# Staging the turned convolution blocks in the filter tiles, and moving their reads and the second heads' values into the next head

## The chip, the cores and the metric

One core of a Trainium2 chip runs the whole layer. It has five engines with a queue each: TensorE (PE in the profile; its weight loads are listed as PEld), VectorE (DVE), ScalarE (ACT), GpSimd (POOL) and SyncE (SP). They run side by side and wait for one another by semaphores; transfers are issued from the queues of SP, ACT and POOL. The metric is the device time of one execution in microseconds, the median of three runs.

## The reference

A decoder layer for 256 tokens of 2048 channels in float32. Two mixers work side by side on the normalised input, 16 heads of attention and a short gated convolution; their projections are gated, added, and projected once more. Cut to what matters:

```python
q_nope, q_rope, k_nope, k_rope, v = ...      # from two 512-wide latents, 16 heads
attn = causal_softmax(q k^T * scale) @ v     # per head: 256 x 256 scores
attn = attn * silu(z_mla)
y_mla = attn @ w_o_mla

u = c_gate * c_in
u_pad = jnp.pad(u, ((0, 0), (CONV_K - 1, 0), (0, 0)))
conv = sum(conv_w[k] * u_pad[:, k:k + s] for k in range(CONV_K))
y_conv = (b_gate * conv * silu(z_conv)) @ w_o_conv

merged = sigmoid(g_mla) * y_mla + sigmoid(g_conv) * y_conv
x = x + rmsnorm(merged @ w_out)
```

## The kernel before

Every product is made to float32 accuracy from two rounded parts: a tile is split into a high part (a copy on ScalarE) and a low part (a subtraction on VectorE) by `split_act` (L232), and three matmuls go for one. The weights come in units of 128 x 2048 (1 MB) through three `raw` buffers on SP's queue, and each unit is split in two halves into `whi` and `wlo`, five buffers each (L186). TensorE's order is written out by hand (`matmul` at L88 keeps program order). For VectorE and ScalarE a scheduler at build time sets the order, save where an instruction is kept in program order; the transfers of POOL discussed here are all kept.

The change lies in the loop over 16 heads (L743 to L804). Each head also carries a sixteenth of the convolution's projections: head h = 4j + n makes the n-th of four products (c_gate, c_in, z_conv, b_gate, in that order) of the j-th block of 512 channels, in four quarters `channels(h, 0..3)` of 24 matmuls. `channels_done` (L689) folds each product into the block in `cv_f` or into `cv_w`. A block has two token halves t of 128 tokens, `cv_t[:, j, t, :]`.

A head from h = 2 on runs so: the gate `z` (`project`, `silu`), `scores(h)`, the quarters of the convolution, with `values` and some steps between, then in odd heads up to 13 the queries and keys of the next pair (`group_a`: matmuls `qn` and `kn`), in heads 3, 7 and 11 the values of the next four heads (`vv`), in even heads `qr`, and the last quarter.

- `scores(h)` (L590) multiplies queries and keys, masks, and makes the softmax in the tile `p` (one buffer).
- `turned(src, via, n)` (L304) turns a tile by a round trip through DRAM: VectorE transposes 32 x 32 blocks into the staging tile `via` (L308); `go` (L311) issues four DMAs from POOL's queue that write it to the tile `far` in DRAM (L315); `come` (L317) issues one DMA from POOL's queue that reads it back (L319) and must wait for the four writes. For `p` the `go` stands in `scores`, the `come` in the loop behind the second quarter.
- `turn(h, p)` (L635) splits the turned scores into `pt` (one buffer), ScalarE's copy and VectorE's subtraction kept in program order.
- `values(h, pt, sz)` (L648) multiplies `pt` by the head's values: four matmuls into the bank `o`, then a copy on ScalarE and an addition and a multiplication on VectorE into `at_f`. In even heads `turn` stands at the end, behind `channels(h, 3)`, and `values` in the next head behind its first quarter. In odd heads both stand in the head itself: `turn` behind the third quarter, `values` behind `group_a`.
- `taps(j, t)` (L706) is the convolution itself for a block's token half, in three parts run at different places: shifted copies of the block into the tiles `mv1` and `mv2` (one buffer each) and two filter rows into tiles `cw` (two buffers), then the products with these and their sum, and the third filter row into `cw`; then the last product and sum. The second half t = 1 starts at the end of head 4j + 1 and is summed in head 4j + 2; the first half t = 0 starts at the end of head 4j + 3 and is summed in head 4j + 4 (the last block's in heads 14 and 15).
- `channels_join(j, t)` (L701) multiplies the convolved block by its gate and turns it in place with `turned_back` (L323): transpose, four writes and the read, one behind the other in POOL's queue. It runs for t = 1 at the end of heads 3, 7, 11 and 15, for t = 0 at the end of heads 4, 8 and 12 and behind the loop. The turned blocks are used after the last head only, in `split_channels` (L825).

All turned tiles of the loop share one staging buffer `via` of 512 columns (L334), but for the very last block, which uses `mv2`.

Of the kernel before, what the change touches and what calls it, by code (L numbers as in the profile page):

```python
# [18 lines left out]
P = 128  # L19
# [63 lines left out]
def tile_layer(ctx: ExitStack, tc: tile.TileContext, xw, x, pos, pvec, post_g, wc, wz, wcv, wkr, wqk, wqr, wv, cwr, wsq, out):  # L83
# [119 lines left out]
    def take(i):  # L203
        ahead(i)
        parts = splits.pop(i)

        def piece(j, n):
            o = j * n
            h, o = o // HALF, o % HALF
            return parts[h][0][:, o : o + n], parts[h][1][:, o : o + n]  # L210

        return piece

    def bank(name, tag="mm", bufs=4):
        return psum.tile([P, 512], F32, name=name, tag=tag, bufs=bufs)

    def product(ps, a, b, first, last):

        (ah, al), (bh, bl) = a, b
        matmul(ps, ah, bh, start=first, stop=False)  # L220
        matmul(ps, ah, bl, start=False, stop=False)
        matmul(ps, al, bh, start=False, stop=last)
# [69 lines left out]
    n = 2 * XW // S  # L292
# [3 lines left out]
    def temp(name, shape=(P, S), dt=F32, bufs=2, tag=None):  # L296

        tag, n = tag or name.rstrip("0123456789_"), shape[-1]
        if n % LINE == 0:
            return bp.tile(list(shape), dt, name=name, tag=tag, bufs=bufs)  # L300
        return bp.tile([P, -(-n // LINE) * LINE], dt, name=name, tag=tag, bufs=bufs)[:, :n]


    def turned(src, via, n):  # L304

        via = via[:, : P * n]
        v = via.rearrange("p (q k x) -> p q k x", q=4, k=n)
        nc.vector.transpose(v.rearrange("p q k x -> p k q x"), src)  # L308
        far = dram.tile([P, P * n], F32, name="far", tag=f"far{n}", bufs=2)

        def go():  # L311
            f = far[:, :].rearrange("(q y) (i m) -> i y q m", q=4, i=4)
            for i in range(4):
                m = via[32 * i : 32 * i + 32, :].rearrange("y (q m) -> y q m", q=4)
                tc.keep_in_program_order(nc.gpsimd.dma_start(out=f[i], in_=m))  # L315

        def come(dst):  # L317

            tc.keep_in_program_order(nc.gpsimd.dma_start(out=dst, in_=far[:, :]))  # L319

        return go, come

    def turned_back(src, via, n):  # L323
        go, come = turned(src, via, n)
        go()
        come(src)

    def by_rows(t, n):
        return t.rearrange("p (i k x) -> p k i x", i=4, k=n)

    def quarters(t):
        return t.rearrange("p k (i x) -> p k i x", i=4)

    def via():  # L334
        return temp("via", (P, 512), bufs=1)


    def split_scaled(dst, src, k):
# [248 lines left out]
    def make(i, j):  # L587
        {"a": group_a, "r": group_r, "v": group_v}[i](j)

    def scores(h):  # L590

        (qn, kn), qr = groups["a", h // HG], groups["r", h // HG]
        j = h % HG
        sc = bank(f"sc{h}", tag="st", bufs=1)
        t0, t1 = slice(0, P), slice(P, S)
        mm = matmul
        o = sc[:, :S].rearrange("p (i k) -> p i k", i=2)
        mm(o, qn[0][:, j, t0], kn[:, :, j, :P], start=True, stop=False)
        mm(sc[:, :P], qn[1][:, j, t0], kn[:, 0, j, :P], start=False, stop=False)
        mm(o, qr[:, j, t0], kr[:, :, :P], start=False, stop=True)  # L600
        o = sc[:, S:]
        product(o, [a[:, j, t1] for a in qn], [kn[:, i, j, :] for i in range(2)], True, False)
        for i in range(2):
            mm(o, qr[:, j, t1], kr[:, i, :], start=False, stop=i == 1)
        if h == 0:
            temp("pad", (P, 4 * LINE), bufs=1)
        p = temp("p", (P, 3 * P), bufs=1)
        half = temp("sc_half", (P, P), bufs=1)
        nc.scalar.activation(half[:, :], sc[:, P:S], AF.Copy)
        nc.vector.tensor_tensor(p[:, :P], sc[:, :P], half[:, :], op=ALU.add)  # L610
        nc.vector.tensor_tensor(p[:, :P], p[:, :P], mask[:, :P], op=ALU.add)
        nc.vector.tensor_tensor(p[:, P:], sc[:, S:], mask[:, P:], op=ALU.add)
        mx, sm, rs = temp("mx", (P, NT)), temp("sm", (P, NT)), temp("rs", (P, NT))
        nb = temp("nb", (P, NT))
        for t in range(NT):
            o = slice(t * P, (2 * t + 1) * P)
            nc.vector.reduce_max(mx[:, t : t + 1], p[:, o], axis=mybir.AxisListType.X)
        nc.vector.tensor_scalar(nb[:, :], mx[:, :], -SCALE, None, op0=ALU.mult)
        for t in range(NT):
            o = slice(t * P, (2 * t + 1) * P)  # L620
            nc.scalar.activation(
                p[:, o], p[:, o], AF.Exp, bias=nb[:, t : t + 1], scale=SCALE,
                accum_out=sm[:, t : t + 1],
            )
        nc.vector.reciprocal(rs[:, :], sm[:, :])
        for t in range(NT):
            o = slice(t * P, (2 * t + 1) * P)
            nc.vector.tensor_scalar(p[:, o], p[:, o], rs[:, t : t + 1], None, op0=ALU.mult)
        if h < 2:
            return p, None  # L630
        go, come = turned(p[:, :], via(), 3)
        go()
        return p, come

# [27 lines left out]
    def silu(name, ps):  # L662
        f, s = temp("sl_f", bufs=1), temp(name)
        whole(f[:, :], ps)
        rows(f[:, :])
        nc.scalar.activation(s[:, :], f[:, :], AF.Sigmoid)
        nc.vector.tensor_tensor(s[:, :], f[:, :], s[:, :], op=ALU.mult)
        return s
# [5 lines left out]
    def channels(h, i, between=None):  # L674

        if i == 0:
            cv_ps["now"] = [bank(f"cv{h}_{t}", tag="cv", bufs=2) for t in range(NT)]
        w = take(u_head[h][1 + i])
        for t in range(NT):
            if t and between:  # L680
                between()
            for k4 in range(4):
                k = 4 * i + k4
                a = [x_both[:, k, o + t * P : o + (t + 1) * P] for o in (0, S)]
                product(cv_ps["now"][t][:, :], a, w(k4, 512), k == 0, k == KD - 1)
        if i == 3:
            channels_done(*divmod(h, 4))
# [13 lines left out]
    def channels_join(j, t):  # L701
        u, w = cv_t[:, j, t, :], cv_w[:, t, :]
        nc.vector.tensor_tensor(u, u, w, op=ALU.mult)
        turned_back(u, via() if t or j < 3 else temp("mv2", (P, 512), bufs=1, tag="mv2x"), 4)

    def taps(j, t):  # L706

# [31 lines left out]
        yield  # L739

    cv_w = bp.tile([P, NT, 512], F32, name="cv_w")
    tap = None
    for h in range(H):  # L743

        tapped = h % 4 == 2 or (h > 0 and h % 4 == 0) or h == H - 1
        sz_new = silu("sz", project(u_head[h][0], f"z{h}"))
        if h == 0:
            latent_turn("qa", qa, "q_g", (("st", 1), ("o", 1)))

            def turn_keys():  # L750
                latent_turn("ckv", ckv, "kv_g", (("mm", 4), ("mm", 4)))
                next(table_parts)

            channels(h, 0, turn_keys)
            for i in first:
                make(*i)
            key_rope()
            channels(h, 1)
            channels(h, 2)
            p, _ = scores(h)  # L760
        elif h == 1:

            pt = turn(0, p)
            channels(h, 0)
            values(0, pt, sz)
            p, _ = scores(h)
            channels(h, 1)
            channels(h, 2)
            pt = turn(h, p)
        else:  # L770
            p, come = scores(h)
            channels(h, 0)
            if h % 2 and h > 2:

                values(h - 1, pt, sz)
            channels(h, 1)
            if tapped:
                next(tap)
            come(p[:, :])
            channels(h, 2)  # L780
            if tapped:
                next(tap)
            if h % 2:
                pt = turn(h, p)
        for i in made[h]:
            make(*i)
            if i[0] == "a":
                values(h, pt, sz_new)
        sz = sz_new
        channels(h, 3)  # L790
        if h > 0 and h % 2 == 0:
            pt = turn(h, p)
        if h == H - 1:
            values(h, pt, sz)
        if h % 4 == 0 and h > 0:
            channels_join(h // 4 - 1, 0)
        if h % 4 == 3:
            channels_join(h // 4, 1)
        if h % 4 == 1:
            tap = taps(h // 4, 1)  # L800
            next(tap)
        elif h % 4 == 3 and h + 1 < H or h == H - 2:
            tap = taps(h // 4, 0)
            next(tap)  # L804
    channels_join(3, 0)


    bstack.close()
# [241 lines left out]
```

## Time and profile before

| | |
|---|---|
| median of three runs | 1059.83 us (1059.41 to 1060.1) |
| the profiled execution | 1060.42 us |
| its span, first to last instruction | 1058.5 us |
| mean granted clock of TensorE | 0.991 |
| VectorE busy | 685.0 us (65%) |
| ScalarE busy | 560.4 us (53%) |
| POOL busy | 155.1 us (15%) |
| heads 0 to 15 | from 52.9 to 613.6 us of the span |

In the profile a busy row gives the time in which an engine had an instruction in it. A wait is named by the engine and line that waited and what released it. A stretch table gives, for each piece of the span, the busy time of the engines and the clock that TensorE was granted, 1.00 being full speed. The chain of waits goes back from an instruction to whatever released it, step by step.

### The profile page before, as it was taken

How to read it: one execution, taken by the hardware profiler on the slowest of the kernel's cores; microseconds unless marked ns; L12 is line 12 of the kernel's file. 1: busy time of each engine (PE TensorE's matmuls, PEld its weight loads, DVE VectorE, ACT ScalarE, POOL GpSimd, SP SyncE). 2: the span in 40 equal slices, each digit the busy share in tenths (PEclk: the TensorE clock that was granted, in tenths of full speed). 3: DMA queues.
4: the chain of work that ended last, by engine and by line, in shares of the span. 5: the costliest groups of instructions: out<-in, count | busy, mean ns of one | idle time of the engine just before them, and what ended most of it. 6: DMA issues, size and time to landing. Idle time of an engine off the chain costs nothing.

```text
span 1058.5 us, 13010 instructions
## 1 busy us (share of the span) xinstructions
PE 1034.1 (98%) x4828; PEld 867.6 (82%) x4828; DVE 685.0 (65%) x984; ACT 560.4 (53%) x770; POOL 155.1 (15%) x297
## 2 busy tenths in 40 slices
PE   9999999998999998999979999999999999999996
PEld 8888888887888887888868888888888888888885
DVE  7588667867677595876857776564464456445562
ACT  7776556665465565655636556444434434443450
POOL 7610021022200321113113120020010002002000
PEclk9999999999999999999989999999999999999998
DMA  8745575577466665665747765565566556558642
GB/s 349 279 169 208 190 233 206 167 260 267 134 219 214 236 234 171 239 214 182 250 175 246 241 238 188 189 225 198 195 213 225 193 189 228 191 194 333 224 159 80
DMA packets 39903, 226.06 MB, mean 214 GB/s; under 512 B 6720, under 2 KB 7424, under 8 KB 16928
## 3 DMA queue, kind: packets, MB, share of 16 engines
q1 hardware_dynamic: 29808, 197.54, 52.7%
q0 software_dynamic: 9600, 24.40, 7.9%
q10 hardware_dynamic: 432, 3.29, 0.8%
q8 instruction: 38, 0.62, 0.2%
q14 instruction: 25, 0.20, 0.1%
HBM read 211.99 MB, written 9.04 MB: 209 GB/s over the span
## 4 chain that ended last, share of the span: by engine, by line
PE 91%; DMA 4%; issue 2%; DVE 2%; POOL 1%; ACT 0%; POOLq 0%; DVEq 0%; ACTq 0%
PE sq L88 33%; PE cv L88 30%; PE z L88 7%; PE out L88 7%; PE vv L88 2%; PE qa L88 2%; PE ckv L88 2%; PE qn L88 2%; DMA far<-via 2%; PE kn L88 2%; PE sc L88 1%; DMA cw<-cwr_dram 1%; PE o L88 1%; PE qr L88 1%; DMA p<-far 1%
## 5 line engine op out<-in xcount | busy, mean ns | idle before, releaser
L234 DVE TENSOR_TENSOR wlo<-raw,whi 128x1024 fp32r<-128x1024 f32 (+1 forms) x370 | 439.4, 1196 | 264.2 <-ACT whi L233 245.7
L233 ACT ACTIVATE whi<-raw 128x1024 fp32r<-128x1024 f32 (+1 forms) x372 | 382.1, 1035 | 372.1 <-PE sq L88 179.8
L88 PE MATMUL cv<-whi,x_both 128*128 128x512 f32 x1024 | 325.0, 392 | 0.0
L88 PEld LDWEIGHTS cv<-whi,x_both 128*128 128x128 f32 x1024 | 194.1, 190 | 39.7
L88 PE MATMUL cv<-wlo,x_both 128*128 128x512 f32 x512 | 200.6, 392 | 0.0
L88 PE MATMUL sq<-whi,x_both 128*128 128x512 f32 x512 | 158.2, 389 | 0.0
L88 PEld LDWEIGHTS cv<-wlo,x_both 128*128 128x128 f32 x512 | 97.2, 190 | 19.0
L88 PEld LDWEIGHTS sq<-whi,x_both 128*128 128x128 f32 x512 | 96.1, 188 | 19.9
L88 PE MATMUL sq<-wlo,x_both 128*128 128x512 f32 x256 | 99.6, 389 | 0.0
L315 POOL DMA_DIRECT2D far<-via x84 | 46.1, 555 | 243.0 <-DVE via L308 240.3
L88 PE MATMUL sq<-whi,cv_both 128*128 128x512 f32 x256 | 79.4, 389 | 0.0
L88 PE MATMUL sq<-whi,at_both 128*128 128x512 f32 x256 | 79.4, 389 | 0.0
L88 PE MATMUL out<-whi,m_both 128*128 128x512 f32 x256 | 79.0, 389 | 0.0
L315 POOL DMA_DIRECT2D far<-sg x32 | 17.4, 551 | 315.1 <-DVE sg L308 241.9
L88 PE MATMUL z<-x_both,whi 128*128 128x512 f32 x256 | 60.7, 389 | 0.0
L88 PEld LDWEIGHTS out<-whi,m_both 128*128 128x128 f32 x256 | 48.1, 188 | 10.0
L88 PEld LDWEIGHTS sq<-whi,cv_both 128*128 128x128 f32 x256 | 48.1, 188 | 10.0
L88 PEld LDWEIGHTS sq<-wlo,x_both 128*128 128x128 f32 x256 | 48.1, 188 | 10.0
L88 PEld LDWEIGHTS sq<-whi,at_both 128*128 128x128 f32 x256 | 48.1, 188 | 10.0
L88 PEld LDWEIGHTS z<-x_both,whi 128*128 128x128 f32 x256 | 48.0, 188 | 9.9
L88 PE MATMUL sq<-wlo,at_both 128*128 128x512 f32 x128 | 49.8, 389 | 0.0
L88 PE MATMUL sq<-wlo,cv_both 128*128 128x512 f32 x128 | 49.8, 389 | 0.0
(216 smaller groups left out, 1127.7 us busy)
## 6 DMA issues: line engine op xcount, KB each, us to landing
raw<-wsq_dram SPq DMA_DIRECT2D x80, 1024.0 KB, 4.7
raw<-wcv_dram SPq DMA_DIRECT2D x64, 1024.0 KB, 5.3
raw<-wz_dram SPq DMA_DIRECT2D x16, 1024.0 KB, 5.0
raw<-wqk_dram SPq DMA_DIRECT2D x8, 1024.0 KB, 4.8
cw<-cwr_dram POOLq DMA_DIRECT2D x24, 256.0 KB, 7.6
raw<-wc_dram SPq DMA_DIRECT2D x4, 1024.0 KB, 10.0
raw<-wv_dram SPq DMA_DIRECT2D x4, 1024.0 KB, 4.7
far<-via POOLq DMA_DIRECT2D x56, 48.0 KB, 4.7
```

Source lines behind the costliest of these rows:

```text
L88: return tc.keep_in_program_order(nc.tensor.matmul(*a, **kw))
L233: a = nc.scalar.activation(hi, src, AF.Copy)
L234: b = nc.vector.tensor_tensor(lo, src, hi.bitcast(F32), op=ALU.subtract)
L315: tc.keep_in_program_order(nc.gpsimd.dma_start(out=f[i], in_=m))
```

## The change

`via` serves the score tiles alone and has 384 columns. `channels_join` stages a block of the second token half in a `cw` tile, one of the first half in `mv2`; it issues the four writes and hands back the read, which the loop issues in the next head, behind `scores` (the last two behind the loop). In heads 5, 9 and 13 `turn` moves behind the last quarter of the head, and `values` into the next head behind its first quarter, as in the even heads. Heads 1, 3, 7, 11 and 15 keep both where they were. `turned_back` and the helper `via` are dropped.

```diff
--- before.py
+++ after.py
@@ -320,19 +320,11 @@
 
         return go, come
 
-    def turned_back(src, via, n):
-        go, come = turned(src, via, n)
-        go()
-        come(src)
-
     def by_rows(t, n):
         return t.rearrange("p (i k x) -> p k i x", i=4, k=n)
 
     def quarters(t):
         return t.rearrange("p k (i x) -> p k i x", i=4)
-
-    def via():
-        return temp("via", (P, 512), bufs=1)
 
 
     def split_scaled(dst, src, k):
@@ -628,7 +620,7 @@
             nc.vector.tensor_scalar(p[:, o], p[:, o], rs[:, t : t + 1], None, op0=ALU.mult)
         if h < 2:
             return p, None
-        go, come = turned(p[:, :], via(), 3)
+        go, come = turned(p[:, :], temp("via", (P, 3 * P), bufs=1), 3)
         go()
         return p, come
 
@@ -701,7 +693,11 @@
     def channels_join(j, t):
         u, w = cv_t[:, j, t, :], cv_w[:, t, :]
         nc.vector.tensor_tensor(u, u, w, op=ALU.mult)
-        turned_back(u, via() if t or j < 3 else temp("mv2", (P, 512), bufs=1, tag="mv2x"), 4)
+
+        via = temp("cw", (P, 512), bufs=2) if t else temp("mv2", (P, 512), bufs=1, tag="mv2x")
+        go, come = turned(u, via, 4)
+        go()
+        return lambda: come(u)
 
     def taps(j, t):
 
@@ -739,7 +735,7 @@
         yield
 
     cv_w = bp.tile([P, NT, 512], F32, name="cv_w")
-    tap = None
+    tap, coming = None, []
     for h in range(H):
 
         tapped = h % 4 == 2 or (h > 0 and h % 4 == 0) or h == H - 1
@@ -769,8 +765,10 @@
             pt = turn(h, p)
         else:
             p, come = scores(h)
+            while coming:
+                coming.pop()()
             channels(h, 0)
-            if h % 2 and h > 2:
+            if h > 2 and h % 4:
 
                 values(h - 1, pt, sz)
             channels(h, 1)
@@ -780,29 +778,31 @@
             channels(h, 2)
             if tapped:
                 next(tap)
-            if h % 2:
+            if h % 4 == 3:
                 pt = turn(h, p)
         for i in made[h]:
             make(*i)
-            if i[0] == "a":
+            if i[0] == "a" and (h == 1 or h % 4 == 3):
                 values(h, pt, sz_new)
         sz = sz_new
         channels(h, 3)
-        if h > 0 and h % 2 == 0:
+        if h > 1 and h % 4 != 3:
             pt = turn(h, p)
         if h == H - 1:
             values(h, pt, sz)
         if h % 4 == 0 and h > 0:
-            channels_join(h // 4 - 1, 0)
+            coming.append(channels_join(h // 4 - 1, 0))
         if h % 4 == 3:
-            channels_join(h // 4, 1)
+            coming.append(channels_join(h // 4, 1))
         if h % 4 == 1:
             tap = taps(h // 4, 1)
             next(tap)
         elif h % 4 == 3 and h + 1 < H or h == H - 2:
             tap = taps(h // 4, 0)
             next(tap)
-    channels_join(3, 0)
+    coming.append(channels_join(3, 0))
+    for come in coming:
+        come()
 
 
     bstack.close()
```

## The prediction

> **What bounds the kernel now.** I read the busy table first, then TensorE's own waits, its timeline at those waits, the busy time per head, and last the chain of waits that ends at the longest of them.
>
> ```profile
> span 1058.5 us, 13010 instructions
> PE 1034.1 (98%) x4828; PEld 867.6 (82%) x4828; DVE 685.0 (65%) x984; ACT 560.4 (53%) x770; POOL 155.1 (15%) x297
> PE o L88 <- DVE pt L234: 13.6, 3, 7.2
> PE idle L88 <- POOL hpi L257: 1.1, 1, 1.1
> ```
>
> TensorE is busy for 98% of the span. Its waits for a named releaser are 1.1 us at the start and 13.6 us in three pieces, all at the attention-values matmul `o`, all for `pt`, the split of the turned score tile. The rest of the 24.4 us of idle time (1058.5 − 1034.1) is the tail behind the last matmul, which the change does not touch. So only the three waits can be won, and anything that makes TensorE wait elsewhere is lost in full. The timeline of TensorE places them in heads 5, 9 and 13:
>
> ```profile
> 264.02 0.47 PE L88 MATMUL o<-pt,vv_hi 128*128 128x512 f32 x1 [2.69 <-DVE pt L234]
> 404.38 0.77 PE L88 MATMUL o<-pt,vv_hi 128*128 128x512 f32 x1 [3.72 <-DVE pt L234]
> 548.25 0.77 PE L88 MATMUL o<-pt,vv_hi 128*128 128x512 f32 x1 [7.23 <-DVE pt L234]
> ```
>
> The first number is the start, the last the idle time before it: 2.69 + 3.72 + 7.23 = 13.64 us. But the waits cost more than they last. The table by stretches (start:end, length, then busy us with counts for PE, PEld, DVE, ACT, POOL, the granted clock, the DMA share, GB/s) for the whole heads 5, 9, 13, and 7 for comparison, then for TensorE alone just behind each wait:
>
> ```profile
> 232.35:271.89 39.54, 36.85 (x177) 31.11 (x177) 29.03 (x53) 22.43 (x36) 6.03 (x11) 0.96 0.57 202
> 371.68:412.24 40.56, 36.84 (x178) 31.18 (x177) 31.68 (x57) 22.37 (x36) 6.58 (x12) 0.96 0.61 211
> 512.03:555.92 43.89, 36.66 (x178) 30.99 (x177) 29.83 (x54) 22.36 (x36) 6.03 (x11) 0.92 0.54 191
> 301.55:342.02 40.47, 40.47 (x201) 34.38 (x201) 30.91 (x53) 24.19 (x39) 2.76 (x5) 1.00 0.58 207
> 331.12 5.46 PE vv L88 x24
> 264.02:267.50 3.48, 3.48 (x11) 0.56 0.01 2
> 404.38:407.80 3.42, 3.42 (x10) 0.50 0.00 0
> 548.25:551.60 3.35, 3.35 (x10) 0.57 0.00 0
> ```
>
> Head 7 does the work of heads 5, 9 and 13 plus the `vv` product, and never waits: 40.47 − 5.46 = 35.01 us is the undisturbed length of such a head. Against it heads 5, 9 and 13 are longer by 4.53, 5.55 and 8.88 us, together **18.96 us**. Of that 13.64 is waiting; the other 5.32 (1.84, 1.83 and 1.65) is TensorE running at a granted clock of 0.50 to 0.57 for some 3.4 us behind each wait.
>
> [...]
>
> **Why `pt` is late there.** The chain that ends at the wait of head 13 (start, us, what):
>
> ```profile
> 522.48 0.56 POOL far L315
> 525.70 1.10 POOL far L315 x2
> 526.80 5.18 DMA far<-via
> 532.56 0.57 POOL cv_f L319
> 533.13 1.62 POOL far L315 x3
> 534.75 6.45 DMA far<-via
> 541.75 5.21 DMA p<-far
> 546.99 0.53 ACT pt L233
> 547.55 0.57 DVE pt L234
> 548.25 0.77 PE o L88
> 532.11 0.58 DVE L308 STREAM_TRANSPOSE via<-p 128x384 f32<-128x384 f32 x1 [2.11 <-DMA far<-via]
> ```
>
> A turned tile makes two trips: four writes to DRAM (L315) and one read back (L319), all in POOL's queue, the read waiting for the writes. The convolution block joined at the end of head 12 is written at 522.5; its read holds POOL until 532.56; only then go the writes of the score tile (533.13), and its read (541.75) lands at 547. The last row is VectorE's: the score tile's transpose too stood 2.11 us, because the one buffer `via` still held the convolution block.
>
> **The change, part by part.** Durations are those of the profiled execution, which took 1060.42 us with its span of 1058.5; it is 0.59 us above the median of the three runs, 1059.83.
>
> (1) *Values of heads 5, 9, 13 move* to the next head, behind that head's z, scores and first quarter of the convolution; their split `pt` moves behind the last quarter of their own head. TensorE's order changes, its work does not. What TensorE now does before it needs `pt`, by head 9's and head 5's rows:
>
> ```profile
> 371.68 5.54 PE z L88 x32
> 377.22 0.95 PE sc L88 x8
> 378.17 5.45 PE cv L88 x24
> 383.62 0.57 PE o L88 x4
> 226.88 5.47 PE cv L88 x24
> 380.36 0.55 DVE L234 TENSOR_TENSOR pt<-p,pt 128x384 fp32r<-128x384 f32 x1
> ```
>
> It is one last quarter (5.47) and z, sc, first quarter (11.94): 17.4 us later. The lateness was at most 7.2, so 10.2 us of cover remain in head 13 and over 13 in the others. All three waits go, and with them the slow clock: −18.96 us. VectorE's and ScalarE's share of the values (one `pt` split, a copy, an add and a multiplication) goes from a full head to a lighter one; it cannot cost TensorE anything unless VectorE becomes the bound (rival 1).
>
> (2) *Reads of convolution blocks move* behind the next head's score writes in POOL's queue. Nothing is added: the four writes and the read are the same. The score tile's writes no longer stand behind the convolution read: in head 13 that is worth up to the 2.5 us from the transpose's earlier start, off TensorE's path after (1), so 0. The other way, the block's read now runs ahead of the score tile's read:
>
> ```profile
> cv_f<-far POOLq DMA_DIRECT2D x8, 256.0 KB, 3.0
> ```
>
> That is 0.57 us to issue and 3.0 to land, so `p` is at most 3.6 us later, which the 10.2 us cover. Without that cover it would cost those 3.6 and one slow clock, 1.84. I take 0. The turned block itself is used only after the last head, and the last two blocks keep their reads at the end, so no reader comes earlier.
>
> (3) *Staging buffers.* `via` serves the scores alone and shrinks from 512 to 384 columns; blocks of the second token half are staged in a `cw` tile, those of the first in `mv2`. The latter is free then: the taps of the block have just been summed out of it. But in heads 3, 7 and 11 the staged block takes one of two `cw` buffers, and the taps that follow want both: the second filter row must wait until the block's writes have landed. POOL waits there, with the next head's score writes behind it. Before, POOL waited for the same landing in the same place, at the block's read (head 7's end):
>
> ```profile
> 346.45 2.17 POOL L315 DMA_DIRECT2D far<-via  x4 [22.33 <-DVE via L308]
> 354.65 0.57 POOL L319 DMA_DIRECT2D cv_f<-far  x1 [6.03 <-DMA far<-via]
> 357.23 1.11 POOL L712 DMA_DIRECT2D cw<-cwr_dram  x2
> DMA to landing us min/median/max: 1.9/4.3/12.4
> ```
>
> The wait ended at 354.65; then came the read, two shifted copies and two fills, and the filter rows at 357.23. Now copies and fills run inside the wait, and the second row goes at about 354.7, some 3 us earlier. That is a gain off the path. Its bad end: the writes land in 12.4 us, the longest in the last row, so the row goes near 361.5, 3.7 us later than its 357.8 before. What hangs on it is the head after, whose `pt` is the next-late thing: in head 9 it is done at 380.91 and wanted at 383.62, a margin of 2.7 us. The bad end thus costs 1.0 us of wait and 1.84 of clock, times three heads: 8.6 us. I take 0, since the usual landing (6.03) is far nearer.
>
> Sum: −18.96 + 0 + 0. Span 1058.5 − 18.96 = 1039.5; that execution 1041.5; from the median 1059.83, **1040.9 us**.
>
> **The rivals.** *1. VectorE becomes the bound in heads 5, 9 and 13* (chance 0.06). For: they hold 29.03, 31.68 and 29.83 us of VectorE work, which the waits let it spread over up to 43.9. The densest stretch that ran without a wait of TensorE is head 15:
>
> ```profile
> 584.18:613.62 29.44, 29.44 (x145) 24.95 (x145) 23.68 (x37) 15.83 (x23) 3.33 (x6) 1.00 0.67 227
> 550.17 0.42 DVE L390 TENSOR_TENSOR at_f<-o,half 128x256 f32<-128x256 f32 x1 [0.49 <-ACT half L389]
> ```
>
> The last row stands for the two operations on `o` that move, 0.42 us each; with `pt`'s 0.55 that takes 1.39 us out of each head: 27.64, 30.29 and 28.44 remain. If 23.68 of 29.44 (0.80) were the highest density VectorE can hold, the heads would last 34.4, 37.7 and 35.4 us against 35.01: 2.7 and 0.4 us of waiting, and 1.84 of slow clock for each of these two, 6.8 together, so **1047.7 us**. Against: TensorE waited for no weight split anywhere in the span (its list of waits has none), and the splits have five buffers each (L186), halves of a unit that occupies TensorE for 5.47 us, so they may run 13.7 us ahead. VectorE's idle time in these heads is largely such waiting for buffers.
>
> *2. The other side: the filter rows wait for the staging buffer* (0.04). Place: POOL's queue at the end of heads 3, 7 and 11, where the second row must wait for the block's writes. VectorE takes the tap products in program order, so while the row is missing it stands there, and the weight splits and the `pt` of the next head behind it. For: the margin there is only 2.7 us. It decides from 18.96 us lost, 6.32 a head: 4.48 of wait and 1.84 of clock, so `pt` 7.2 us later and the row at 365.0, which is 16.4 us behind the end of the writes' issue (348.62). At 20 us it would be 3.6 worse in each of three heads: 1059.83 + 10.8 = **1070.6 us**. Against: no write in the trace took over 12.4 us, and the row goes out behind fewer transfers than before.
>
> *3. The change doesn't do what it says* (0.02): `pt` is late by 17.4 us more, and the same waits stand in heads 6, 10 and 14: **1059.8 us**. It needs ScalarE or VectorE to take the split far behind the arrival of `p`. Against: heads 4, 8 and 12 already run in just this order, and their `o` (383.62) waits for nothing.
>
> **How the numbers follow.** The forecast, all three waits gone and no new one, has 0.88. Its own range is 1039.5 to 1044: below, the spread of the runs shown (1059.41 to 1060.1, so 0.4 down) and up to a microsecond of gain that I don't see, since nothing but the start, the tail and these waits is there to be won; above, the bad end of (3) in one head (2.9). The whole range, 1039.3 to 1048, takes in rival 1; rivals 2 and 3 lie outside, with 0.06. A measurement of this kernel tells from no change what exceeds about 0.2%, 2.1 us. The forecast and rival 1 are faster by 12 us and more: 0.94. Rival 3 is no change: 0.02. Rival 2 is slower: 0.04.
>
> **What would show it.** In the profile of the changed kernel TensorE's waits should hold no `o <- pt` row; heads 5, 9 and 13, from z to z, should last 35.0 us each at a granted clock of 1.00; TensorE's busy time should fall by 5.3 us to about 1028.8 with the same 4828 matmuls. The score tile's writes in heads 5, 9 and 13 should follow their transpose at once, and no transpose into `via` should wait for a DMA. The first wait to look for, if the time is above 1043, is at `o` of heads 4, 8 and 12 (in heads 5, 9 and 13), behind a filter row (L712) issued later than 11 us after the block's writes; then at a weight split in the three heads. The forecast is wrong if TensorE shows a new wait of over 2 us, or if the heads are 35 us and the gain is given back behind 613 us, where the last head now ends.

## The result, and the profile after

The changed kernel takes 1041.97 us (median of four runs, 1041.61 to 1042.68), beside 1059.96 us for the kernel before on the same chip: a ratio of 0.9826 (95% interval 0.9809 to 0.9844). The forecast was 1040.9 us. The page's first two lines and TensorE's waits after:

```profile
span 1040.8 us, 13001 instructions
PE 1029.4 (99%) x4828; PEld 863.7 (83%) x4828; DVE 686.2 (66%) x984; ACT 559.6 (54%) x770; POOL 155.2 (15%) x297
PE idle L88 <- POOL hpi L257: 1.1, 1, 1.1
PE qa L88 <- ACT whi L233: 0.6, 1, 0.6
```

The three waits at `o` are gone. What is left are waits in the first 10 us. Heads 5, 9 and 13 after (stretch, length, PE, PEld, DVE, ACT, POOL, clock, DMA share, GB/s):

```profile
233.44:267.89 34.45, 34.45 (x173) 29.33 (x173) 26.41 (x45) 22.04 (x35) 6.00 (x11) 1.00 0.63 212
368.30:402.75 34.45, 34.45 (x173) 29.32 (x173) 26.58 (x46) 21.75 (x35) 5.99 (x11) 1.00 0.63 213
503.15:537.61 34.46, 34.46 (x174) 29.34 (x173) 25.74 (x44) 21.98 (x35) 6.01 (x11) 1.00 0.60 210
```

They are the undisturbed 35.01 us less the 0.57 of `o`, which now stands in the head after, at full clock. But VectorE's time in them also fell, by 2.6, 5.1 and 4.1 us, where only 1.39 were to move. So something else changed in them. It shows in POOL's queue and on VectorE around head 8, which starts at 338.64 in this profile (342.02 before), head 9 at 368.30 (371.68). The timelines of POOL and VectorE after, and last TensorE's `o` of head 8 from the chain:

```profile
343.06 2.17 POOL L315 DMA_DIRECT2D far<-cw  x4 [23.68 <-DVE cw L308]
...
347.25 0.56 POOL L708 DMA_DIRECT2D cw<-cwr_dram  x1
352.13 0.56 POOL L708 DMA_DIRECT2D cw<-cwr_dram  x1 [4.32 <-issue]
352.67 2.21 POOL L315 DMA_DIRECT2D far<-via  x4
353.86 0.69 DVE L724 TENSOR_TENSOR mv<-mv,cw 128x512 f32<-128x512 f32 x1 [1.13 <-DMA cw<-cwr_dram]
359.57 0.69 DVE L724 TENSOR_TENSOR mv<-mv,cw 128x512 f32<-128x512 f32 x1 [1.15 <-DMA cw<-cwr_dram]
371.43 0.56 DVE L234 TENSOR_TENSOR pt<-p,pt 128x384 fp32r<-128x384 f32 x1 [0.33 <-ACT pt L233]
384.64 0.57 DVE L308 STREAM_TRANSPOSE via<-p 128x384 f32<-128x384 f32 x1
380.23 0.57 PE o L88 x4
```

VectorE's same two products and the transpose of head 9 before:

```profile
368.12 0.69 DVE L728 TENSOR_TENSOR mv<-mv,cw 128x512 f32<-128x512 f32 x1 [2.25 <-DMA cw<-cwr_dram]
369.96 0.69 DVE L728 TENSOR_TENSOR mv<-mv,cw 128x512 f32<-128x512 f32 x1 [1.14 <-DMA cw<-cwr_dram]
391.30 0.58 DVE L308 STREAM_TRANSPOSE via<-p 128x384 f32<-128x384 f32 x1
```

Counted from the head's start, the filter rows are issued 8.6 and 13.5 us in, where both went from 15.2 on before (357.23), and the products with them run at 15.2 and 20.9 us instead of 26.1 and 27.9. Before, they fell into the crowd at the end of head 8; after, they are done by then, and VectorE reaches the transpose of head 9's scores 16.3 us into that head instead of 19.6. The margin at `o` of head 8 grew from 2.7 to 8.2 us (371.99 to 380.23). In heads 5, 9 and 13 the score tile's read goes out 23.7, 22.5 and 21.1 us into the head, where it was 25.8, 27.4 and 29.7.

The forecast's sum held nearly whole: from the first z to the end of the last head's `o` the kernel went from 560.73 to 541.94 us, 18.79 for the 18.96 forecast. The 1.08 us between that and the span's 17.7 is lost ahead of the first z, in code that the change leaves alone. The start of the first z, from the chains of waits, after and before:

```profile
1.65 6.03 DMA raw<-xw_dram
53.97 5.55 PE z L88 x32
```

```profile
52.89 5.55 PE z L88 x32
```

In the profiles of the nine runs below that leave the computation as it is, that start lies between 53.13 and 53.95; the profile that the sum was made from happened to start earliest of all.

### The profile page after: what moved, and what is told of

Its sections match the earlier page's. It is cut to its first block, busy times and chain, and to the rows that moved or that the text cites. A ratio compares the mean times of both kernels' runs of the same rounds, so it can differ in the third digit from the quotient of the medians.

```text
span 1040.8 us, 13001 instructions
## 1 busy us (share of the span) xinstructions
PE 1029.4 (99%) x4828; PEld 863.7 (83%) x4828; DVE 686.2 (66%) x984; ACT 559.6 (54%) x770; POOL 155.2 (15%) x297
## 4 chain that ended last, share of the span: by engine, by line
PE 97%; issue 1%; DMA 1%; DVE 0%; ACT 0%; SPq 0%; POOLq 0%; POOL 0%; DVEq 0%; ACTq 0%
PE cv L88 34%; PE sq L88 33%; PE z L88 9%; PE out L88 7%; PE kn L88 2%; PE qn L88 2%; PE vv L88 2%; PE ckv L88 2%; PE qa L88 2%; PE sc L88 1%; PE qr L88 1%; PE o L88 1%; DMA raw<-xw_dram 1%; PE kr L88 0%; DVE og L937 0%
## 5 line engine op out<-in xcount | busy, mean ns | idle before, releaser
L315 POOL DMA_DIRECT2D far<-via x56 | 30.8, 556 | 142.1 <-DVE via L308 142.1
```

## The experiments

The question was how much of the gain is the move of the values (theory 1, the forecast's) and how much the earlier arrival of the score tile, which the forecast had counted as nothing (theory 2). Each run was compared with the kernel before on its own chip; that kernel's runs spread from 1057.95 to 1067.82 us there, so the ratios count. "Own heads" means that `turn` and `values` of heads 5, 9 and 13 stand where they stood before.

| run | us (range) | ratio (95%) | waits at `o` in its profile |
|---|---|---|---|
| e1 values moved alone | 1042.72 (1042.22 to 1045.97) | 0.9813 (0.9784 to 0.9842) | 2.0, head 15 |
| e2 staging and later reads, own heads | 1043.22 (1042.62 to 1044.13) | 0.9820 (0.9795 to 0.9845) | none |
| e3 staging alone, own heads | 1059.24 (1055.62 to 1062.81) | 0.9961 (0.9942 to 0.9981) | 2.69, 7.06, 4.83 |
| e4 later reads alone, own heads | 1044.78 (1042.24 to 1051.43) | 0.9844 (0.9799 to 0.9889) | 3.09, head 5 |
| e5 second halves' reads later, own heads | 1042.76 (1042.54 to 1042.85) | 0.9818 (0.9790 to 0.9845) | none |
| e6 first halves' reads later, own heads | 1059.54 (1057.17 to 1063.18) | 0.9979 (0.9957 to 1.0001) | 2.69, 4.44, 3.21 |
| e7 one buffer for the filter rows | 1042.32 (1041.98 to 1042.66) | 0.9814 (0.9771 to 0.9856) | none |
| e8 pauses | 1132.81 | | |
| e9 reads behind the rows, own heads | 1048.68 (1045.61 to 1052.5) | 0.9891 (0.9844 to 0.9937) | 1.95, 1.97 |
| e10 rows behind the writes, own heads | 1055.22 (1054.07 to 1059.59) | 0.9935 (0.9908 to 0.9962) | 2.69, 2.69, 2.69 |

**Which half?** e1 is the kernel before with the diff's conditions on `turn` and `values` and nothing else of it.

```diff
-            if h % 2 and h > 2:
+            if h > 2 and h % 4:
...
-            if h % 2:
+            if h % 4 == 3:
...
-            if i[0] == "a":
+            if i[0] == "a" and (h == 1 or h % 4 == 3):
...
-        if h > 0 and h % 2 == 0:
+        if h > 1 and h % 4 != 3:
```

> The kernel before with the move of turn and values of heads 5, 9 and 13 alone; staging and reads as before. Theory 1 (the forecast's): the move alone takes all three waits, 1041 to 1042 us, no wait at o. Theory 2 (either half of the change is enough, since the staging also brings the score tile earlier): the same here. Rival: without the earlier filter rows the thin margin of 2.7 us at o of head 8 (in head 9) gives way, one to three waits of 1 to 3 us with 1.8 of slow clock each, 1045 to 1052.

e2 is the changed kernel with these four conditions put back.

> The changed kernel with turn and values of heads 5, 9 and 13 put back into their own heads: staging in the filter tiles and later reads alone. Theory 1 (the forecast's part 2: worth up to 2.5 us, in head 13): waits of about 2.7, 3.7 and 4.7 us stay, 1057 us. Theory 2: the read of the score tile goes out 2.0, 4.9 and 8.6 us earlier in heads 5, 9 and 13 (23.7, 22.5 and 21.1 us from the head's start in the changed kernel, 25.8, 27.4 and 29.7 before), which leaves at most 0.7 us of waiting in head 5: 1042 to 1045.

Each half alone gives the whole gain. Theory 1's number for e2 (1057) is out by 14 us; theory 2's fits. e2's heads 5, 9 and 13:

```profile
233.68:268.86 35.18, 35.18 (x178) 29.93 (x177) 26.91 (x47) 22.29 (x36) 6.00 (x11) 1.00 0.60 208
368.65:403.81 35.16, 35.16 (x178) 29.93 (x177) 27.62 (x49) 22.23 (x36) 6.00 (x11) 1.00 0.60 207
503.61:538.77 35.16, 35.16 (x177) 29.93 (x177) 27.68 (x48) 22.23 (x36) 6.01 (x11) 1.00 0.62 213
```

With the values in their own heads these last 35.2 us and no wait is left. e1's rival looked at the margin at `o` of head 8: in e1's profile `pt` is done at 377.86 and `o` starts at 379.62, so 1.8 us were left of the 2.7, and it held. The one wait of that profile is at another place, head 15's own `o`, which the change doesn't move. TensorE's timeline there, and then the stretch behind the wait (stretch, length, PE, clock, DMA share, GB/s), in which the granted clock was 0.70:

```profile
596.72 0.47 PE L88 MATMUL o<-pt,vv_hi 128*128 128x512 f32 x1 [1.99 <-DVE pt L234]
```

```profile
596.72:600.10 3.38, 3.38 (x12) 0.70 0.04 17
```

**Buffer or place of the read?** e3 is e2 with each read directly behind its writes again; e4 is e2 with the blocks staged in the shared `via`, again of 512 columns.

```diff
         go()
-        return lambda: come(u)
+        come(u)
+        return lambda: None
```

> As the run before, but each block's read stands directly behind its writes again: the other staging tiles alone. Theory 1: only the 2.1 us that the score tile's transpose stood for the shared buffer in head 13 go, 1057 us. Theory 2: the read and the copies hold POOL as before, so the filter rows come no earlier, 1056 to 1058; if it comes out below 1050, the buffer alone was what kept the score tile late.

```diff
-        via = temp("cw", (P, 512), bufs=2) if t else temp("mv2", (P, 512), bufs=1, tag="mv2x")
+        via = temp("via", (P, 512), bufs=1) if t or j < 3 else temp("mv2", (P, 512), bufs=1, tag="mv2x")
```

> As e2, but all blocks are staged in the shared via of 512 columns again: the later reads alone. Theory 1: nothing is won, 1059 to 1060. Theory 2: the filter rows go out some 3 us earlier and the score tile's writes no longer stand behind the block's read; the transpose still waits for the buffer in head 13 (2 us), so one or two waits of 1 to 3 us stay, 1044 to 1050.

The staging alone wins 0.4%, which fits neither theory better than the other. The later reads alone win most of what e2 wins, as theory 2 said. The buffer is of little use by itself; what it adds to the reads isn't settled, since e4's four runs lie between 1042.24 and 1051.43 us.

**Which reads?** e5 and e6 are e2 with only the one or the other half's reads issued later.

```diff
         go()
+        if t == 0:
+            come(u)
+            return lambda: None
         return lambda: come(u)
```

> As e2_reads (values in their own heads), but only the reads of the second token halves, joined at the end of heads 3, 7 and 11, are issued later; those of the first halves (heads 4, 8, 12) stand behind their writes again. Theory rows: what counts is that the filter rows go out earlier, so VectorE reaches the next head's transpose 2 to 4 us earlier; all of e2's gain stays, 1042 to 1046 us, no wait or one of under 2 us at o. Theory order: what counts is that the score tile's writes no longer stand behind the block's read in heads 5, 9 and 13; then nothing is won, 1057 to 1060.

e6 has `t == 1` there.

> The other part: only the reads of the first token halves are issued later. Theory rows: heads 5 and 9 keep their waits (2.7 and 3.7 us), head 13 loses some 2.5 of its 7.2 because POOL is free for the score tile's writes: 1055 to 1059 us. Theory order: all gain is here, 1042 to 1046.

That decides it: all of the gain is in the reads at the end of heads 3, 7 and 11, and none that can be measured in those of heads 4, 8 and 12, which alone stand ahead of the late score tiles of heads 5, 9 and 13 in POOL's queue. Heads 5, 9 and 13 of e5, then of e6:

```profile
233.41:268.56 35.15, 35.15 (x177) 29.92 (x177) 26.90 (x47) 22.32 (x36) 6.03 (x11) 1.00 0.61 206
368.36:403.49 35.13, 35.13 (x177) 29.92 (x177) 28.03 (x49) 22.11 (x36) 6.02 (x11) 1.00 0.62 213
503.28:538.44 35.16, 35.16 (x178) 29.92 (x177) 26.85 (x47) 22.23 (x36) 6.04 (x11) 1.00 0.61 212
```

```profile
232.97:272.51 39.54, 36.85 (x177) 31.10 (x177) 29.52 (x54) 22.21 (x36) 6.32 (x12) 0.96 0.58 210
372.30:413.56 41.26, 36.82 (x178) 31.16 (x177) 31.77 (x57) 22.37 (x36) 6.56 (x12) 0.96 0.58 206
513.36:553.43 40.07, 36.85 (x177) 31.17 (x177) 31.55 (x56) 22.37 (x36) 6.58 (x12) 0.96 0.59 213
```

**Rows or writes?** At the end of heads 3, 7 and 11 two things stand behind the read: the filter rows, and behind them the score writes of the head that follows. e9 puts the reads between the two, e10 puts the copies and rows last.

```diff
             tap = taps(h // 4, 0)
             next(tap)
+            while coming:
+                coming.pop()()
```

> As e2_reads (values in their own heads), but the reads of the second halves stand at the end of heads 3, 7 and 11 directly behind the copies and the two filter rows, ahead of the score tile's writes. Theory rows: the rows still go out as early as in e2, so all of the gain stays, 1042 to 1046 us. Theory writes: what counted in e2 was that the next head's score writes went ahead of the block's read; then the waits of heads 5 and 9 come back, 1052 to 1059.

```diff
             while coming:
                 coming.pop()()
+            if h % 4 == 0:
+                next(tap)
...
             tap = taps(h // 4, 0)
-            next(tap)
+            if h == H - 2:
+                next(tap)
```

> As e2_reads, but the copies and the filter rows of the first halves (started at the end of heads 3, 7 and 11) are issued in the next head, behind the score tile's writes and the block's read. Theory rows: the rows go out some 6 us later than in e2, near their time in the kernel before or past it, and the waits of heads 5, 9 and 13 come back, 1052 to 1060 us. Theory writes: the score tile's writes go first, so the gain stays, 1042 to 1046.

e10 has the score writes first and loses 12 us of e2's gain; e9 has the rows first and keeps some 60% of it. Both point to the rows, but neither is clean. e9's time lies between the two expectations, with two waits of 2 us in its profile, before which ScalarE stood for the score tile:

```profile
397.22 0.52 ACT L233 ACTIVATE pt<-p 128x384 fp32r<-128x384 f32 x1 [2.79 <-DMA p<-far]
```

The rows had done their part there: head 9's transpose ran 16.6 us into the head, nearly as early as in e2 (16.2; 18.0 in e10, 19.6 before). But then POOL stood 5.1 us for the tile's writes to land, where it stood 1.4 in e2. Why they took longer is open.

In e10 the waits are not the tile's: ScalarE stands for it in none of the three heads. They come from the order in which ScalarE and VectorE take their work, set when the kernel is built. ScalarE in head 9 of e10, then of e2:

```profile
402.35 0.37 ACT L381 ACTIVATE half<-kn 128x256 f32<-128x256 f32 x1
402.62 0.52 ACT L233 ACTIVATE pt<-p 128x384 fp32r<-128x384 f32 x1
394.90 0.64 ACT L381 ACTIVATE half<-qn 128x256 f32<-128x256 f32 x2
395.42 0.53 ACT L233 ACTIVATE pt<-p 128x384 fp32r<-128x384 f32 x1
```

In e10 the copy of the tile stands behind those of the keys' products `kn`, which TensorE makes last before `o`; so `o` waits 2.69 us even for a tile that has landed. In e2 it stands ahead of them. Heads 5, 9 and 13 have the first order in the kernel before, e3, e6 and e10, and the second in e2, e4, e5 and e9. So the runs that keep the gain and the runs that lose it differ in this order too, and how the gain divides between the order and the earlier tile is not shown. Both matter: with the first order and no standing for the tile, e10's three heads are together 11.6 us longer than e2's; with the second order and the read of the tile 25.6 us into the head, head 5 of e4 waits 3.09.

**The second row made later.** e7 gives the filter rows one buffer, and the staged block one of its own.

```diff
-        via = temp("cw", (P, 512), bufs=2) if t else temp("mv2", (P, 512), bufs=1, tag="mv2x")
+        via = temp("cv_via", (P, 512), bufs=1) if t else temp("mv2", (P, 512), bufs=1, tag="mv2x")
...
-            cw = temp("cw", (P, 512), bufs=2)
+            cw = temp("cw", (P, 512), bufs=1)
```

> The changed kernel with one buffer for the filter rows and a buffer of its own for the staged block, so that each second row waits until the product with the first is done: the wait of the forecast's rival 2, made longer, at the end of every head with new taps. The row goes out some 6 us later and POOL's queue with it. By the forecast's price, wait = lateness minus margin, and the margin at o of head 8, which was 2.7 us before, is 8.2 us in the changed kernel (371.99 to 380.23): no wait, 1041 to 1044 us. If VectorE standing for the row starves the weight splits, TensorE shows waits for wlo and the time is 1050 or more; if the lateness is 10 us or more, waits at o of 2 us and more with 1.8 of slow clock each, 1046 to 1062.

POOL's second row, then VectorE's second product and `pt` of head 8, which starts at 338.49, and TensorE's `o`:

```profile
353.56 0.56 POOL L708 DMA_DIRECT2D cw<-cwr_dram  x1 [5.89 <-DVE mv L724]
```

```profile
362.62 0.69 DVE L724 TENSOR_TENSOR mv<-mv,cw 128x512 f32<-128x512 f32 x1 [4.35 <-DMA cw<-cwr_dram]
374.55 0.55 DVE L234 TENSOR_TENSOR pt<-p,pt 128x384 fp32r<-128x384 f32 x1
380.08 0.57 PE o L88 x4
```

The row came 1.6 us later from the head's start than in the changed kernel, not 6; `pt` came 3.3 us later (36.61 us in, 33.35 after the change), and the margin shrank to 5.0. No wait follows, as expected, but the test was weaker than meant: it shows that the margin takes 3 us, not that it takes 6.

**The slow clock.** e8 puts pauses of growing length into the heads.

```python
def gap(h):
    ps, g = bank(f"gap{h}"), temp("gap", (P, S), bufs=1)
    matmul(ps[:, :P], ones[:, :], ones[:, :], start=True, stop=True)
    tc.keep_in_program_order(nc.vector.tensor_copy(g[:, :P], ps[:, :P]))
    for _ in range(h - 2):
        tc.keep_in_program_order(nc.vector.tensor_tensor(g[:, :P], g[:, :P], g[:, :P], op=ALU.max))
    matmul(ps[:, P:S], ones[:, :], g[:, :P], start=True, stop=True)
```

> The changed kernel with a pause of TensorE put into each head from 2 to 15, behind the second quarter of the convolution: a small matmul, a chain of 1 to 14 short VectorE operations on its result, and a small matmul that reads the end of the chain. It adds 28 matmuls whose results are not used. It measures the slow clock against the length of the idle time before it. Theory flat: each pause from about 2 us on costs the same 1.6 to 1.9 us beyond its length, as the waits before did (2.69, 3.72, 7.23 us: 1.84, 1.83, 1.65). [...]

Four of its pauses on TensorE's timeline, and the quarter of the convolution behind each in the chain (5.47 us undisturbed):

```profile
185.76 0.49 PE L88 MATMUL gap<-gap,ones 128*128 128x128 f32 x2 [2.44 <-DVE gap L745]
229.13 0.78 PE L88 MATMUL gap<-gap,ones 128*128 128x128 f32 x2 [2.77 <-DVE gap L745]
264.85 0.49 PE L88 MATMUL gap<-gap,ones 128*128 128x128 f32 x2 [3.09 <-DVE gap L745]
303.47 0.49 PE L88 MATMUL gap<-gap,ones 128*128 128x128 f32 x2 [3.42 <-DVE gap L745]
```

```profile
186.25 5.47 PE cv L88 x24
229.91 6.80 PE cv L88 x24
265.34 5.47 PE cv L88 x24
303.96 7.09 PE cv L88 x24
```

Theory flat falls: pauses of 1.08, 2.44 and 3.09 us cost nothing beyond their length (the granted clock was 1.00 in the 3.40 us behind each), that of 2.77 cost 1.6 us (0.51), and all ten from 3.42 to 6.36 us cost between 1.3 and 2.8 (0.50 to 0.62), with no order in it by length (from the pause's end to the start of the 24th matmul of the convolution: 5.58 us undisturbed, 6.91 to 8.36 slow).

## Why the prediction was right, and where a step was not

**(1) The move of the values** did what the forecast said: all three waits and the slow clock behind them went (1.00 in heads 5, 9 and 13, where it was 0.96, 0.96 and 0.92), and e1 has it alone at a ratio of 0.9813. In heads 5, 9 and 13 `pt` is done 9.8 us before the `o` that now stands in the next head; the forecast had counted on 10.2 or more. The size of 18.96 us measured 18.79; TensorE's busy time fell to 1029.4 us for the 1028.8 forecast. A detail was wrong: the heads last 34.45 us, not 35.0, since `o` leaves them.

**(2) The later reads** are the step that failed. It counted them as worth up to 2.5 us, in head 13, because the score tile's writes would no longer stand behind the block's read. Without (1) they give the whole gain together with the other staging tiles (e2, e5) and most of it alone (e4). As (1) takes the same waits, counting them as nothing left the sum right; the sum doesn't test this term. Two readings led there. First, the chain of waits was shown for head 13 alone and taken for all three. In head 5 it has no DMA in it:

```profile
261.39 0.40 ACT qn_hi L233
261.78 0.27 ACT half L389
262.05 0.30 ACT qn_hi L233
262.36 0.28 ACT half L389
262.66 0.75 DVE qn_lo L234 x2
263.41 0.48 DVE pt L234
```

There `pt` waits behind the splits of the next pair's queries, in the order that was set when the kernel was built, as in e10. Of the 13.64 us of waiting before, three times 2.69, 8.07 us, would have stood in that order with any tile; the late tile adds the other 5.57. The order alone, with nothing else changed, wasn't tried. Second, the block's read that mattered was another one, a head earlier. A price was off too: the block's read landed after 6.5 us (median in the profile after), not 3.0, so "at most 3.6 us later" was too low; the 9.8 us would cover that as well, and the score tile's reads went out earlier, not later.

**(3) The staging buffers.** The wait at the second filter row was seen in its place, and "some 3 us earlier" was right for the second row by the profile (13.5 us into the head for 15.8, so 2.3); the first row, which the step didn't price, went 6.6 us earlier. "A gain off the path" holds beside (1), since e1 does without it, but not alone: e5 and e6 show that the path to the score tiles of heads 5, 9 and 13 starts at what stands behind the reads of heads 3, 7 and 11. That it is the rows is likely (e9's early transposes, e10), with the order as said above left in. By way of what: VectorE's products with the rows move out of the end of the head, as the profile above shows for head 8. The bad end did not come: POOL stood 3.6, 4.3 and 4.0 us ahead of the second row in heads 4, 8 and 12 (for the 4.3 the profile names no releaser).

**The rivals.** VectorE became no bound: it holds 26.58 us in head 9, not the 30.29 that rival 1 took, for the same reason. Rival 2 has no trace: the margin that it lived on grew to 8.2 us. Rival 3 fell with the waits. The medians fell by 17.99 us for the 18.96 forecast; 0.17 of the difference is in the heads. Whether the rest is the start stays open, since the executions behind the medians have no profile.

## What to carry to other kernels

In POOL's queue a read that waited for its own writes held everything behind it (6.0 us at the end of head 7 before, with the filter rows going out behind it at 357.23); look at what that is, and who waits for it one or two stages on, not only at what the read itself delivers. When a late result shows the same wait in several places, follow the chain at each of them: here one was a queue, and one was the order of two engines. Compare that order between two runs before a difference is put down to a transfer: an edit to one queue can change it. And when two parts of a change aim at one wait, price each alone; a sum that comes out right can hide that either would have done, and what the second buys is margin (8.2 us for 2.7).

## What the runs showed of the hardware

From 1.95 to 3.09 us, the length of a pause didn't settle whether the slow clock followed it. Waits of 1.95 and 1.97 us (e9, its heads at a clock of 1.00) and a pause of 2.44 (e8, 1.00 in the 3.40 us behind it) were followed by none; 1.99 us (e1, 0.70 in the 3.38 us behind it) and 2.77 (e8, 0.51 in 3.40) were. The wait of 2.69 us was followed by it in five places (head 5 of the kernel before, of e3 and of e6, heads 5 and 9 of e10), where `o` and the quarter of the convolution behind it took 7.79 to 7.90 us, and not in a sixth (head 13 of e10, 6.27). 3.09 us was in e4 (7.85 us for the same) and wasn't in e8 (1.00). The three heads of e10:

```profile
233.07:272.65 39.58, 36.89 (x178) 31.09 (x177) 28.65 (x50) 22.18 (x36) 7.12 (x13) 0.96 0.59 200
372.44:411.98 39.54, 36.85 (x178) 31.06 (x177) 29.04 (x51) 22.09 (x36) 7.12 (x13) 0.96 0.59 202
511.77:549.71 37.94, 35.25 (x178) 29.92 (x177) 29.34 (x52) 22.21 (x36) 7.14 (x13) 1.00 0.62 211
```

The same wait of 2.69 us stands in heads of 39.5 us and in one of 37.9. Every pause of 3.42 us and more in e8 was followed by the slow clock, and so were the waits of 3.72 and 7.23 us before (0.50 and 0.57). What decided it for the shorter ones is not shown.
